# Another road into the 2x2 product: two plain blocks first, conditioning beside it, a small inversion on GpSimd

## Chip, core and metric

One core of a Trainium2 chip runs the whole program in one launch. The metric is the device time in microseconds (us). The kernel before was run three times; one further execution was recorded by the hardware profiler, and all rows below come from it.

## What is computed

Two layers of a hybrid backbone over 1152 tokens (128 context and 1024 latent) of width 1024. Cut to what matters here:

```python
m = silu(cond) @ w_ada + b_ada          # per layer: 6 vectors of 1024, for two conditionings (ctx, lat)
h = modulate(rms_norm(x, g), m[0], m[1])
x = x + m[2] * mix(h)                   # layer 0: neighbourhood + differential attention
                                        # layer 1: retention + RWKV-7 scan in both directions
h = modulate(rms_norm(x, g), m[3], m[4])
g, u = split(h @ w_ffn_in)              # D_FF = 2816
x = x + m[5] * ((silu(g) * u) @ w_ffn_out)
# at the end one rms_norm; fp32 throughout
```

## The kernel before

TensorE works in fp32r: every fp32 operand is split into a high and a low part (a cast on ScalarE and a subtraction on VectorE or GpSimd), and each product is three matmuls. The program is written as generators and ordered by a list scheduler when it is built: the order on each engine is fixed in advance by planned times, and each engine's queue then runs in that order and waits where something is late. DMAs are issued from SyncE's queue (SP) in one order too.

The parts that the diff touches, in order of time:

- **Layer 0's conditioning**, column groups 4 to 11 of 512 columns (`ada_steps`, lines 187 to 203), beside the differential attention. A step loads a [128 x 512] tile of `w_ada` (`aw`, line 133), splits it (ScalarE line 140, GpSimd line 141) and issues two matmuls with four stationary columns (line 148). After 8 steps `ada_end` copies the [4 x 512] sum and turns it (line 160). `pull` gives 0.28 steps per slot.
- **FFN of each layer** (`ffn`, lines 1656 to 1821). `w_ffn_in` is worked through in 22 column blocks f. Block 0 is plain: `mm3` over 8 row tiles for 3 token groups of 384 columns and for gate and up, 144 matmuls. From block 1 on, a Winograd-like 2x2 scheme makes 7 products instead of 8: each product is 24 matmuls of 288 columns, so 168 in a block. It needs combinations of the activations, which `forms` (lines 1823 to 1867) makes once on VectorE, GpSimd and ScalarE in 24 units: T1 and T2 (8 units), T3 (8) and a last sum (8) that overwrites a part of `hH`, `hL`. Each product is taken out of PSUM banks A, B, E, D by ScalarE and VectorE. Results go to DRAM (`hdr`).
- **FFN out** (`ffn_out`, lines 1869 to 1928) reads `hdr` and `w_ffn_out` through the ring of 6 `raw` tiles, 1584 matmuls of 384 columns. In layer 0, layer 1's conditioning runs beside it (`ada_vec`, lines 205 to 232): per step one `aw` tile out of the same ring, two VectorE operations that add it, times a scalar, to `aacc`; every 8 steps 8 fp32 matmuls with a column of ones (line 230).
- **Layer 1's scan** (`rec_scan`): 18 rounds m of `prep`, `amat`, `inv16`, `values`, `levels`, `chain`, interleaved by a written order. `inv16` (lines 1220 to 1256) inverts 16x16 triangular blocks: the blocks go to DRAM and come back block by partition (`bts`, `BT`), a copy (line 1232), 15 rounds of a multiplication (line 1241) and an addition (line 1242) on VectorE with at most 64 elements in a partition, a copy and an addition (lines 1244 and 1245), and again through DRAM (`mbs`, `ML`). `BT` and `MB` have one buffer each.

```python
for j in range(15):
    nc.vector.tensor_tensor(tt, row, col, op=ALU.mult)
    nc.vector.tensor_tensor(M3[:, j + 1 :, :ncl], M3[:, j + 1 :, :ncl], tt, op=ALU.add)
```

Of the kernel before, what the change touches and what calls it, by code (L numbers as in the profile page):

```python
# [44 lines left out]
class Net:  # L45
# [41 lines left out]
    def setup(self, top):  # L87
# [32 lines left out]
        self.cond = self.t(c, [P, KT, 4], F32R, tag="cond")  # L120
        cv = self.v2[:, 0:16].rearrange("p (c k) -> p k c", c=2)
        self.split(self.cond[:, :, 0::2], self.cond[:, :, 1::2], cv)
        self.comb = self.t(c, [4, 2], tag="comb")
        nc.scalar.dma_start(self.comb, I["k_comb"])
# [11 lines left out]
    def ada_split(self, w, n, pool, eng=None):  # L136
        nc = self.nc
        wh = self.t(pool, [P, n, 512], F32R, tag="awh")
        wl = self.t(pool, [P, n, 512], F32R, tag="awl")
        nc.scalar.copy(wh, w)  # L140
        (eng or nc.gpsimd).tensor_tensor(wl, w, wh, op=ALU.subtract)  # L141
        return wh, wl

    def ada_mm(self, pt, k, n, ws):
        wh, wl = ws
        for i in range(n):
            for ww in (wh, wl):
                self.nc.tensor.matmul(
                    pt[0:4, :], lhsT=self.cond[:, k + i, :], rhs=ww[:, i, :], start=k + i == 0 and ww is wh, stop=k + i == KT - 1 and ww is wl
                )  # L150

    def ada_end(self, l, cg, pt, pool, ps, r=4):

        nc = self.nc
        s4 = self.t(pool, [r, 512], tag="as4", bufs=1)
        nc.scalar.copy(s4, pt[0:r, :])
        p2 = self.t(ps, [P, 512], tag="mm")
        comb = self.comb if r == 4 else self.ident[0:2, 0:2]
        for f in range(4):
            nc.tensor.matmul(p2[:, 2 * f : 2 * f + 2], lhsT=s4[:, f * P : (f + 1) * P], rhs=comb, start=True, stop=True)  # L160
        self.ada_mod(l, cg, p2)
# [14 lines left out]
    def ada(self, l, cg, pool, ps, n):  # L176

        pt = self.t(ps, [P, 512], tag="mm")
        cond = self.v2[:, 0:16].rearrange("p (c k) -> p k c", c=2)
        for k in range(0, KT, n):  # L180
            w = self.ada_load(l, cg, k, n, pool)
            for i in range(k, k + n):
                self.nc.tensor.matmul(pt[0:2, :], lhsT=cond[:, i, :], rhs=w[:, i - k, :], start=i == 0, stop=i == KT - 1)
        self.ada_end(l, cg, pt, pool, ps, 2)

    def ada_steps(self, l, cgs, pool, ps, eng=None):

        seq = [(cg, k) for cg in cgs for k in range(KT)]
        raw, spl, pt = {}, {}, None
        for i in range(-3, len(seq)):  # L190
            if i + 3 < len(seq):
                raw[i + 3] = self.ada_load(l, *seq[i + 3], 1, pool)
            if 0 <= i + 2 < len(seq):
                spl[i + 2] = self.ada_split(raw.pop(i + 2), 1, pool, eng)
            if i >= 0:
                cg, k = seq[i]
                if k == 0:
                    pt = self.t(ps, [P, 512], tag="ada")
                self.ada_mm(pt, k, 1, spl.pop(i))
                if k == KT - 1:  # L200
                    self.ada_end(l, cg, pt, pool, ps)
                yield

    def ada_vec(self, l, cgs, pool):


        nc = self.nc
        seq = [(cg, k) for cg in cgs for k in range(KT)]
        raw, acc = {}, None
        for i in range(-1, len(seq)):  # L210
            if i + 1 < len(seq):
                raw[i + 1] = self.ada_load(l, *seq[i + 1], 1, pool)
            if i < 0:
                continue
            cg, k = seq[i]
            w = raw.pop(i)[:, 0, :]
            if k == 0:
                acc = self.t(pool, [P, 2, 512], tag="aacc", bufs=1)
            for c in range(2):
                s = self.v2[:, c * 8 + k : c * 8 + k + 1]  # L220
                if k == 0:
                    nc.vector.tensor_scalar_mul(acc[:, c, :], w, s)
                else:
                    nc.vector.scalar_tensor_tensor(acc[:, c, :], w, s, acc[:, c, :], op0=ALU.mult, op1=ALU.add)  # L224
            if k == KT - 1:
                p2 = self.t(self.nps, [P, 512], tag="mm")
                for f in range(4):
                    for c in range(2):
                        o = p2[:, 2 * f + c : 2 * f + c + 1]
                        nc.tensor.matmul(o, lhsT=acc[:, c, f * P : (f + 1) * P], rhs=self.ones, start=True, stop=True)  # L230
                self.ada_mod(l, cg, p2)
            yield

# [827 lines left out]
    def rec_scan(self, hp):  # L1061
        nc, I, O = self.nc, self.I, self.O
        hp.release()
        with ExitStack() as es:
# [155 lines left out]
            def inv16(m):  # L1220
# [16 lines left out]
                for j in range(15):  # L1237
# [3 lines left out]
                    nc.vector.tensor_tensor(tt, row, col, op=ALU.mult)  # L1241
                    nc.vector.tensor_tensor(M3[:, j + 1 :, :ncl], M3[:, j + 1 :, :ncl], tt, op=ALU.add)  # L1242
# [413 lines left out]
    def ffn(self, l, x, hH, hL, p, tp, cs, ps, side, last):  # L1656
# [24 lines left out]
        cw = {}  # L1681
        for u in range(2):
            for a in range(2):
                w, c = raw(0, a, u), slice((u * 2 + a) * 512, (u * 2 + a + 1) * 512)
                cw[u, a] = T["T3h"][:, c], T["T3l"][:, c]
                self.split(*cw[u, a], w)
        forms = self.forms(hH, hL, ops, _Cycle(cs), p)
        pg = []
        for tg in range(TG):
            sl = slice(tg * GW, (tg + 1) * GW)  # L1690
            for u in range(2):
                pt = self.t(ps, [P, 512], tag="mm")
                for k in range(KT):
                    wh, wl = (w[:, (k % 4) * P : (k % 4 + 1) * P] for w in cw[u, k // 4])
                    self.mm3(pt[:, :GW], wh, wl, hH[k][:, sl], hL[k][:, sl], k == 0, k == KT - 1)
                pg.append(pt)
                self.tail_step()
        for tg in range(TG):
            for _ in itertools.islice(forms, (4, 2, 2)[tg]):
                pass  # L1700
            s = self.t(p, [P, GW], tag="c")
            nc.scalar.activation(s, pg[2 * tg][:, :GW], AF.Silu)
            nc.vector.tensor_tensor(s, s, pg[2 * tg + 1][:, :GW], op=ALU.mult)
            nc.sync.dma_start(self.hdr[0][:, tg * GW : (tg + 1) * GW], s)
# [52 lines left out]
        load(1, (0, 0), (1, 0), (0, 1), (1, 1))  # L1757
        prep(1, 0)
        prep(1, 1)
        seq = [(f, i) for f in range(1, NF) for i in range(7)]  # L1760
        out2 = self.ffn_out(l, x, hH, hL, p, T, ps, wo, side, last)
        C, store = {}, []
# [55 lines left out]
        for d, s in store:  # L1818
            nc.sync.dma_start(d, s)
        for _ in out2:  # L1820
# [143 lines left out]
    def run(self):  # L1964
        tc, nc, I = self.tc, self.nc, self.I
        self.tail = iter(())
        with ExitStack() as top:
# [8 lines left out]
            def ahead():  # L1976
                wp = wes.enter_context(self.pool("wA", side="right"))
                self.wpool = _Bufs(wp, {"wraw": 3, "wh": 9, "wl": 9, "ist": 2, "aw": 2, "awh": 3, "awl": 3})
# [21 lines left out]
    def attn(self, hp, hH, hL, wes):  # L2000
# [16 lines left out]
        GS, AS, OS = 0.28, 0.28, 0.34  # L2017
# [5 lines left out]
        with ExitStack() as es:  # L2023
            ps = _Mux(_Bufs(es.enter_context(self.pool("psA", space=PSUM)), {"S": 1, "ada": 1}), bps, ("mm", "T", "o"), {"S": "bba"})
# [7 lines left out]
            ada = self.ada_steps(0, range(4, 12), wpool, ps)  # L2032
# [258 lines left out]
```

## Time and profile before

| | |
|---|---|
| runs, median (lowest to highest) | 3959.39 us (3959.38 to 3960.79) |
| the profiled execution, its own time | 3954.28 us |
| its span | 3952.3 us |
| mean granted TensorE clock | 0.964 |
| busy: TensorE, VectorE, ScalarE, GpSimd | 94%, 60%, 37%, 28% |

Busy time is the union of an engine's instructions. A matmul's row spans its whole way through the array, so matmuls overlap and a busy TensorE is not one at its peak; counts of matmuls in a stretch tell more. The granted clock is a share of 2.4 GHz (0.5 is the lower level of 1.2 GHz).

### The profile page before, as it was taken

Reading aid. Unit: us, or ns where it says so; the run is one execution under the profiler, and the core shown is the slowest. Engines: PE = TensorE matmul, PEld = TensorE weight load, DVE = VectorE, ACT = ScalarE, POOL = GpSimd, SP = SyncE. Lnnn points to the kernel's source line nnn. Section 1 sums busy time; section 2 is a strip of 40 time slices with the busy share of each in tenths; the row PEclk is TensorE's granted clock in tenths of the full one; section 3 lists DMA queues with packets and bytes.
Section 4 is the critical chain, followed back from the end, with each engine's and each line's share of the span. In section 5 each row is a group of like instructions: output and inputs, shape, how many; then the busy total and the mean of one; then the engine's idle time right before and its main releaser. Section 6 shows DMA issues by size and latency. Waiting matters only on the chain.

```text
span 3952.3 us, 67315 instructions
## 1 busy us (share of the span) xinstructions
PE 3709.5 (94%) x24997; PEld 3465.6 (88%) x24997; DVE 2362.6 (60%) x5461; ACT 1457.2 (37%) x3454; POOL 1128.2 (29%) x1064
## 2 busy tenths in 40 slices
PE   8999998999899999999999997888888989999998
PEld 5899997999799999999989886777767879999998
DVE  5566665666744448885253657888875774444434
ACT  4555545555333341115222323232222533334221
POOL 3322202103532233332020322233332453223430
PEclk9999998999899999999999997999998989999999
DMA  6532316431122225543333435222223112222431
GB/s 204 151 101 83 106 56 157 128 94 49 51 77 73 76 87 171 166 149 114 102 118 98 167 103 167 70 63 74 68 52 96 51 54 74 73 78 89 127 91 60
DMA packets 425695, 392.16 MB, mean 99 GB/s; under 512 B 68212, under 2 KB 370672, under 8 KB 423832
## 3 DMA queue, kind: packets, MB, share of 16 engines
q1 hardware_dynamic: 406928, 376.29, 31.2%
q10 hardware_dynamic: 13160, 7.27, 0.7%
q0 software_dynamic: 5280, 4.31, 0.5%
q8 instruction: 197, 3.23, 0.3%
q14 instruction: 130, 1.06, 0.1%
HBM read 289.32 MB, written 98.33 MB: 98 GB/s over the span
## 4 chain that ended last, share of the span: by engine, by line
PE 54%; DVE 12%; DMA 5%; issue 2%; POOL 1%; ACT 1%; SPq 0%; DVEq 0%; ACTq 0%; POOLq 0%
PE mm L82 6%; PE mm L84 6%; PE mm L83 6%; PE A L1745 3%; PE A L1747 3%; PE A L1746 3%; PE E L1747 2%; PE E L1745 2%; PE E L1746 2%; DVE c L1827 1%; PE mm L858 1%; DVE MB L1242 1%; PE mm L860 1%; PE mm L859 1%; PE A L1191 1%
## 5 line engine op out<-in xcount | busy, mean ns | idle before, releaser
L770 DVE SCALAR_TENSOR_TENSOR x<-mm,mod,x 128x128 f32<-128x128 f32 (+1 forms) x576 | 278.9, 511 | 213.5 <-PE mm L84 212.3
L1677 POOL TENSOR_TENSOR wl<-raw,wh 128x512 fp32r<-128x512 f32 x126 | 172.1, 1366 | 588.3 <-ACT wh L1676 584.0
L1676 ACT CAST wh<-raw 128x512 fp32r<-128x512 f32 x294 | 182.2, 620 | 346.6 <-PE A L1746 123.1
L391 PE MATMUL mm<-wh,hH 128*128 128x384 f32 x576 | 199.1, 346 | 3.0 <-ACT ist L409 3.0
L392 PE MATMUL mm<-wl,hH 128*128 128x384 f32 x576 | 195.1, 339 | 0.0
L393 PE MATMUL mm<-wh,hL 128*128 128x384 f32 x576 | 193.7, 338 | 0.0
L75 DVE TENSOR_TENSOR wl<-wraw,wh 128x256 fp32r<-128x256 f32 (+1 forms) x184 | 95.7, 540 | 114.2 <-ACT wh L74 86.4
L82 PE MATMUL mm<-hH,wh 128*128 128x384 f32 x432 | 152.5, 354 | 2.8 <-ACT wh L74 2.8
L1191 PE MATMUL A<-AR,BK 64*128 64x256 f32 x576 | 125.6, 438 | 30.5 <-DVE tf L1241 11.1
L84 PE MATMUL mm<-hH,wl 128*128 128x384 f32 x432 | 148.7, 346 | 2.9 <-DVE rst L908 2.4
L1719 DVE TENSOR_TENSOR raw<-raw,raw 128x512 f32<-128x512 f32 x42 | 30.9, 737 | 200.8 <-POOL raw L1718 200.8
L1677 DVE TENSOR_TENSOR wl<-raw,wh 128x512 fp32r<-128x512 f32 x168 | 120.1, 715 | 48.6 <-ACT wh L1676 46.5
L224 DVE SCALAR_TENSOR_TENSOR aacc<-aw,v,aacc 128x512 f32<-128x512 f32 x168 | 148.7, 920 | 0.0
L82 PE MATMUL mm<-mh,owh 128*128 128x384 f32 x384 | 141.1, 382 | 7.6 <-ACT mh L74 5.3
L83 PE MATMUL mm<-hL,wh 128*128 128x384 f32 x432 | 148.1, 344 | 0.0
L84 PE MATMUL mm<-mh,owl 128*128 128x384 f32 x384 | 133.5, 348 | 2.0 <-DVE owl L75 2.0
L83 PE MATMUL mm<-ml,owh 128*128 128x384 f32 x384 | 135.4, 353 | 0.0
L141 POOL TENSOR_TENSOR awl<-aw,awh 128x512 fp32r<-128x512 f32 x64 | 88.2, 1387 | 158.5 <-ACT awh L140 107.0
L1191 PEld LDWEIGHTS A<-AR,BK 64*128 64x128 f32 x576 | 82.2, 208 | 55.0 <-issue 15.5
L1790 DVE TENSOR_TENSOR c<-c,B 128x288 f32<-128x288 f32 x84 | 38.1, 454 | 153.5 <-PE B L1747 83.4
L565 ACT ACTIVATE P<-S,mx 128x384 f32<-128x384 f32 (+1 forms) x200 | 111.9, 569 | 45.6 <-DVE mx L563 45.6
L858 PE MATMUL mm<-wh,hH 128*128 128x256 f32 x432 | 124.0, 290 | 0.0
(553 smaller groups left out, 13019.2 us busy)
## 6 DMA issues: line engine op xcount, KB each, us to landing
raw<-in_w_ffn_in_dram SPq DMA_DIRECT2D x176, 256.0 KB
aw<-in_w_ada_dram SPq DMA_DIRECT2D x160, 256.0 KB
raw<-hdr SPq DMA_DIRECT2D x132, 192.0 KB
hdr<-c SPq DMA_DIRECT2D x168, 144.0 KB
raw<-in_w_ffn_out_dram SPq DMA_DIRECT2D x88, 256.0 KB
F<-stg SPq DMA_DIRECT2D x34, 640.0 KB
stg<-st SPq DMA_DIRECT2D x12, 1536.0 KB
qkv<-ist SPq DMA_DIRECT2D x72, 192.0 KB
```

What stands on the lines that cost most here:

```text
L82: mm(out, lhsT=wh, rhs=xh, start=first, stop=False)
L83: mm(out, lhsT=wh, rhs=xl, start=False, stop=False)
L84: mm(out, lhsT=wl, rhs=xh, start=False, stop=last)
L391: mm(pt[:, :ncol], lhsT=hH[k][:, c], rhs=WH[k], start=k == 0, stop=False)
L392: mm(pt[:, :ncol], lhsT=hH[k][:, c], rhs=WL[k], start=False, stop=False)
L393: mm(pt[:, :ncol], lhsT=hL[k][:, c], rhs=WH[k], start=False, stop=k == KT - 1)
L770: self.nc.vector.scalar_tensor_tensor(x[f][:, c], pt[:, a:b], self.mod[l][jg][:, f, cd : cd + 1], x[f][:, c], op0=ALU.mult, op1=ALU.add)
L1191: mm(pts[h][:, j * 256 : j * 256 + 256], lhsT=BK[hs, j, :], rhs=AR[hs], start=True, stop=True)
L1677: eng.tensor_tensor(wl, w, wh, op=ALU.subtract)
L1745: mm(o, lhsT=wh[:, ks], rhs=xh, start=new and k == 0, stop=False, skip_group_check=True)
L1746: mm(o, lhsT=wh[:, ks], rhs=xl, start=False, stop=False, skip_group_check=True)
L1747: mm(o, lhsT=wl[:, ks], rhs=xh, start=False, stop=k == 3, skip_group_check=True)
```

## The change

Four edits. (1) Layer 0's conditioning runs as `ada_vec` on VectorE, at 0.3 steps per slot, with two `aw` tiles; its PSUM bank goes to the attention's scores `S`. (2) The FFN's block 1 is plain too, and the forms are spread over both plain blocks and the first 2x2 products; the 2x2 scheme starts at block 2; the loads for the next block are regrouped. (3) Layer 1's conditioning runs beside the 2x2 products from block 3 on, at 0.82 steps per product, no longer beside FFN out; it has one `aw` tile of its own, layer 0's `raw` ring has 5 tiles, and the sum of a column group uses PSUM bank D. `ada_vec` loads the next tile after the operations of the last, and reads a finished sum one step later. (4) The two operations of the inversion's rounds are issued on GpSimd.

```diff
@@ ada_vec
-        for i in range(-1, len(seq)):
-            if i + 1 < len(seq):
-                raw[i + 1] = self.ada_load(l, *seq[i + 1], 1, pool)
...
+        w, acc, p2 = self.ada_load(l, cgs[0], 0, 1, pool), None, None
+        for n, cg in enumerate(cgs):
+            for k in range(KT):
+                if k == 0:
+                    if p2 is not None:
+                        self.ada_mod(l, cgs[n - 1], p2)
+                    acc = self.t(pool, [P, 2, 512], tag="aacc", bufs=1)
+                for c in range(2):
+                    s = self.v2[:, c * 8 + k : c * 8 + k + 1]
+                    if k == 0:
+                        nc.vector.tensor_scalar_mul(acc[:, c, :], w[:, 0, :], s)
+                    else:
+                        nc.vector.scalar_tensor_tensor(acc[:, c, :], w[:, 0, :], s, acc[:, c, :], op0=ALU.mult, op1=ALU.add)
+                if k < KT - 1 or n < len(cgs) - 1:
+                    w = self.ada_load(l, *((cg, k + 1) if k < KT - 1 else (cgs[n + 1], 0)), 1, pool)
+                yield
+            p2 = self.t(self.nps, [P, 512], tag="mm")
...
@@ inv16
-                    nc.vector.tensor_tensor(tt, row, col, op=ALU.mult)
-                    nc.vector.tensor_tensor(M3[:, j + 1 :, :ncl], M3[:, j + 1 :, :ncl], tt, op=ALU.add)
+                    nc.gpsimd.tensor_tensor(tt, row, col, op=ALU.mult)
+                    nc.gpsimd.tensor_tensor(M3[:, j + 1 :, :ncl], M3[:, j + 1 :, :ncl], tt, op=ALU.add)
@@ ffn (third, evac: the plain block as before, as functions)
+        w0 = [split(raw(1, a, 0), nc.vector) for a in range(2)]
         for tg in range(TG):
-            for _ in itertools.islice(forms, (4, 2, 2)[tg]):
-                pass
...
+            evac(0, tg, *pg[2 * tg : 2 * tg + 2])
+            form((4, 2, 0)[tg])
+        pg = [third(w0, tg) for tg in range(TG)]
+        w1 = [split(raw(1, a, 1), nc.vector) for a in range(2)]
+        form(4)
+        for tg in range(TG):
+            pu = third(w1, tg)
+            form(2)
+            evac(1, tg, pg[tg], pu)
...
-        seq = [(f, i) for f in range(1, NF) for i in range(7)]
+        seq = [(f, i) for f in range(2, NF) for i in range(7)]
...
+        self.nps = _Alias(ps.pool, {"mm": "D"})
...
-            for _ in itertools.islice(forms, 4):
-                pass
+            form(3)
...
-            elif i == 2:
-                load(f + 1, (1, 0))
             elif i == 5:
-                load(f + 1, (0, 1), (1, 1))
+                load(f + 1, (1, 0), (0, 1), (1, 1))
+            if n >= 7:
+                due += 0.82
+                while due >= 1:
+                    due -= 1
+                    next(side, None)
@@ attn
-        GS, AS, OS = 0.28, 0.28, 0.34
+        GS, AS, OS = 0.28, 0.3, 0.34
-            ps = _Mux(_Bufs(es.enter_context(self.pool("psA", space=PSUM)), {"S": 1, "ada": 1}), bps, ("mm", "T", "o"), {"S": "bba"})
+            ps = _Mux(_Bufs(es.enter_context(self.pool("psA", space=PSUM)), {"S": 2}), bps, ("mm", "T", "o"), {"S": "ba"})
-            ada = self.ada_steps(0, range(4, 12), wpool, ps)
+            ada = self.ada_vec(0, range(4, 12), wpool)
@@ ffn_block
-            p = _Bufs(es.enter_context(self.pool(f"ff{l}", "right" if l else "left")), {"raw": 6, "wh": 3, "wl": 3, "c": 4})
+            p = _Bufs(es.enter_context(self.pool(f"ff{l}", "right" if l else "left")), {"raw": 6 if l else 5, "wh": 3, "wl": 3, "c": 4})
-            side = iter(()) if l else self.ada_vec(1, range(12), _Alias(p, {"aw": "raw"}))
+            side = iter(()) if l else self.ada_vec(1, range(12), p)
```

## Rows read from the trace of the kernel before

**Rows 1.** The page: span, engines' busy us; a group's count, busy us, mean ns.

```profile
span 3952.3 us, 67315 instructions
...
PE 3709.5 (94%) x24997; PEld 3465.6 (88%) x24997; DVE 2362.6 (60%) x5461; ACT 1457.2 (37%) x3454; POOL 1128.2 (29%) x1064
...
L224 DVE SCALAR_TENSOR_TENSOR aacc<-aw,v,aacc 128x512 f32<-128x512 f32 x168 | 148.7, 920 | 0.0
```

**Rows 2.** Windows: stretch, length, busy us (instructions), granted clock, DMA share, GB/s.

```profile
110.00:590.00 480.00, 465.59 (x2960) 440.46 (x2961) 305.16 (x754) 252.43 (x766) 105.56 (x98) 0.99 0.33 99
990.00:1040.00 50.00, 32.27 (x163) 28.59 (x162) 47.49 (x67) 16.72 (x39) 34.51 (x34) 0.73 0.08 24
1050.00:1480.00 430.00, 430.00 (x3235) 429.60 (x3235) 189.74 (x347) 161.67 (x335) 131.18 (x100) 1.00 0.25 78
1490.00:1785.00 295.00, 282.46 (x1601) 280.07 (x1602) 242.21 (x398) 57.20 (x105) 99.73 (x82) 0.95 0.51 160
2425.00:2955.00 530.00, 461.70 (x3641) 379.72 (x3642) 436.85 (x1296) 150.16 (x351) 160.75 (x172) 0.95 0.23 61
3160.00:3210.00 50.00, 32.11 (x154) 28.77 (x152) 46.64 (x67) 17.08 (x40) 33.93 (x34) 0.73 0.08 24
3660.00:3910.00 250.00, 250.00 (x1444) 250.00 (x1443) 100.62 (x198) 51.26 (x96) 83.63 (x79) 1.00 0.29 87
```

**Rows 3.** The chain that ended last, 2839 to 2872 us: start, us, what.

```profile
2840.39 0.28 DVE BT L1244
...
2841.92 3.35 DMA mbs<-BT
...
2846.30 1.78 DMA BT<-bts
...
2848.20 1.00 DVE BT L1232
...
2870.57 0.28 DVE BT L1244
```

**Rows 4.** Lines 1232 and 1241: count, ns min/median/max, first and last start.

```profile
L1232 DVE COPY BT<-BT x18: 283/620/1257, 2421.9 to 2936.5; 32x256 f32<-32x256 f32 x18
...
L1241 DVE TENSOR_TENSOR tf<-BT,MB x270: 155/201/1265, 2423.2 to 2951.8; 64x15 f32<-64x15 f32 x18, 64x39 f32<-64x39 f32 x18, 64x55 f32<-64x55 f32 x18, 64x63 f32<-64x63 f32 x18
```

**Rows 5.** GpSimd's groups by form, 2425 to 2955 us: busy us, mean ns, idle before.

```profile
L1168 POOL TENSOR_TENSOR BK<-F,EN 128x512 f32<-128x512 f32 x30 | 38.8, 1295 | 128.4 <-ACT BH L1171 50.3 <-issue 40.7 <-ACT X L1278 26.0
...
L1166 POOL TENSOR_TENSOR AR<-F,EL 128x256 f32<-128x256 f32 x30 | 22.3, 742 | 34.7 <-PE c L1337 34.7
```

**Rows 6.** Timeline, 2604 to 2608 us, VectorE and GpSimd: start, us.

```profile
2606.50 0.73 POOL L1166 TENSOR_TENSOR AR<-F,EL 128x256 f32<-128x256 f32 x1 [0.89 <-PE c L1337]
...
2606.57 0.72 DVE L1241 TENSOR_TENSOR tf<-BT,MB 64x48 f32<-64x48 f32 x1
```

**Rows 7.** TensorE's waits, 940 to 1060 us: total, times, longest.

```profile
PE A L1745 <- ACT T3h L1856: 8.5, 1, 8.5
```

**Rows 8.** Groups of instructions, 100 to 600 us: count, busy us, mean ns.

```profile
L148 PE MATMUL ada<-awl,cond 128*4 128x512 f32 x64 | 25.5, 398 | 1.3 <-POOL awl L141 1.1
...
L160 PE MATMUL mm<-comb,as 4*128 4x2 f32 x64 | 8.4, 249 | 1.9 <-ACT ist L409 1.9
```

**Rows 9.** Timeline of TensorE, 1702 to 1708 us.

```profile
1704.29 1.84 PE L230 MATMUL mm<-ones,aacc 128*128 128x1 f32 x16
1705.99 0.42 PE L82 MATMUL mm<-T3h,hH 128*128 128x384 f32 x1
```

**Rows 10.** Line 224 on VectorE: count, ns min/median/max, first and last start.

```profile
L224 DVE SCALAR_TENSOR_TENSOR aacc<-aw,v,aacc x168: 732/743/1831, 1485.6 to 1766.3; 128x512 f32<-128x512 f32 x168
```

**Rows 11.** Timelines of SyncE's queue and ScalarE, 330 to 360 us.

```profile
335.82 0.34 SPq L133 DMA_DIRECT2D aw<-in_w_ada_dram  x1
...
339.07 0.62 ACT L140 CAST awh<-aw 128x512 fp32r<-128x512 f32 x1 [2.29 <-DMA aw<-in_w_ada_dram]
```

**Rows 12.** SyncE's own waits, 1480 to 1790 us: total, times, longest.

```profile
SPq L133 <- DMA raw<-hdr: 16.0, 14, 2.8
```

More of the change, by code (lines that the diff above doesn't have):

```diff
@@ L134, in ada_load, with ada_end @@
         return w
-    def ada_split(self, w, n, pool, eng=None):
+    def ada_end(self, l, cg, pt, pool, ps):
         nc = self.nc
[L138 to L156, printed above, removed]
+        s2 = self.t(pool, [2, 512], tag="as2", bufs=1)
+        nc.scalar.copy(s2, pt[0:2, :])
         p2 = self.t(ps, [P, 512], tag="mm")
-        comb = self.comb if r == 4 else self.ident[0:2, 0:2]
+        comb = self.ident[0:2, 0:2]
         for f in range(4):
-            nc.tensor.matmul(p2[:, 2 * f : 2 * f + 2], lhsT=s4[:, f * P : (f + 1) * P], rhs=comb, start=True, stop=True)
+            nc.tensor.matmul(p2[:, 2 * f : 2 * f + 2], lhsT=s2[:, f * P : (f + 1) * P], rhs=comb, start=True, stop=True)
         self.ada_mod(l, cg, p2)
@@ L183, in ada @@
                 self.nc.tensor.matmul(pt[0:2, :], lhsT=cond[:, i, :], rhs=w[:, i - k, :], start=i == 0, stop=i == KT - 1)
[L184 to L202, printed above, removed]
+        self.ada_end(l, cg, pt, pool, ps)
@@ new lines, in ada_vec @@
+        w, acc, p2 = self.ada_load(l, cgs[0], 0, 1, pool), None, None
+        for n, cg in enumerate(cgs):
+            for k in range(KT):
+                if k == 0:
+                    if p2 is not None:
[11 more added lines that the diff above has]
+            p2 = self.t(self.nps, [P, 512], tag="mm")
+            for f in range(4):
+                for c in range(2):
+                    o = p2[:, 2 * f + c : 2 * f + c + 1]
+                    nc.tensor.matmul(o, lhsT=acc[:, c, f * P : (f + 1) * P], rhs=self.ones, start=True, stop=True)
@@ L232, in ada_vec @@
             yield
+        self.ada_mod(l, cgs[-1], p2)
     @staticmethod
@@ L1678, in split, with evac, third, form @@
             return wh, wl
-        cw = {}
+        def evac(f, tg, g, u):
+            s = self.t(p, [P, GW], tag="c")
+            nc.scalar.activation(s, g[:, :GW], AF.Silu)
+            nc.vector.tensor_tensor(s, s, u[:, :GW], op=ALU.mult)
+            nc.sync.dma_start(self.hdr[f][:, tg * GW : (tg + 1) * GW], s)
+        def third(w, tg):
+            pt = self.t(ps, [P, 512], tag="mm")
+            sl = slice(tg * GW, (tg + 1) * GW)
+            for k in range(KT):
+                wh, wl = (v[:, (k % 4) * P : (k % 4 + 1) * P] for v in w[k // 4])
+                self.mm3(pt[:, :GW], wh, wl, hH[k][:, sl], hL[k][:, sl], k == 0, k == KT - 1)
+            return pt
+        def form(n):
+            for _ in itertools.islice(forms, n):
+                pass
+        cw = [[], []]
         for u in range(2):
@@ L1689, in ffn @@
         for tg in range(TG):
-            sl = slice(tg * GW, (tg + 1) * GW)
             for u in range(2):
[L1692 to L1696, printed above, removed]
+                pg.append(third(cw[u], tg))
                 self.tail_step()
+        w0 = [split(raw(1, a, 0), nc.vector) for a in range(2)]
         for tg in range(TG):
-            for _ in itertools.islice(forms, (4, 2, 2)[tg]):
-                pass
[L1701 to L1704, printed above, removed]
+            evac(0, tg, *pg[2 * tg : 2 * tg + 2])
[7 more added lines that the diff above has]
+            evac(1, tg, pg[tg], pu)
         cs = _Cycle(cs)
@@ L1756, in ffn @@
         wo = I["w_ffn_out"][l]
-        load(1, (0, 0), (1, 0), (0, 1), (1, 1))
-        prep(1, 0)
-        prep(1, 1)
-        seq = [(f, i) for f in range(1, NF) for i in range(7)]
+        load(2, (0, 0), (1, 0), (0, 1), (1, 1))
+        prep(2, 0)
+        prep(2, 1)
+        seq = [(f, i) for f in range(2, NF) for i in range(7)]
         out2 = self.ffn_out(l, x, hH, hL, p, T, ps, wo, side, last)
-        C, store = {}, []
+        C, store, due = {}, [], 0.0
+        self.nps = _Alias(ps.pool, {"mm": "D"})
         H2 = HT // 2
```

35 lines of the change are left out of this document (5 added, 30 removed).

## The prediction

> **What bounds the kernel now.** I read the page first: TensorE is busy 94% of the span [rows 1], but that is a mean over stages, so I cut the span into stretches. In the windows [rows 2] the reader should compare the count of matmuls, not the busy time. In the FFN's 2x2 products (1050 to 1480) TensorE runs without a gap at clock 1.00: 430 us / 3235 = 0.133 us per matmul of 288 columns; layer 1's FFN out (3660 to 3910) does the same, 250 / 1444 = 0.173 us per matmul of 384. These two are the full rates. Against them three places lose time.
>
> First, the beginning of both FFNs: 163 matmuls in 50 us (990 to 1040) where the full rate needs 163 x 0.133 = 21.7 us, so 28.3 us are lost, and in layer 1 (3160 to 3210) 154, so 29.5 us. VectorE is busy 47.5 of these 50 us; the largest single wait of TensorE is 8.5 us for T3 [rows 7], and its clock in the stretch is 0.73, so it fell to the lower level after such gaps. Second, layer 0's FFN out (1490 to 1785) has VectorE at 82% and TensorE's clock at 0.95; of its 1601 matmuls 192 are the narrow ones of line 230. Third, layer 1's scan: TensorE 87%, VectorE 82%.
>
> For the scan I read the chain [rows 3]: from the copy out of one inversion (2840.39) through two DMAs to the copy into the next (2848.20) are 7.8 us, and the inversion itself takes until 2870.57, 22.4 us, because its 30 short operations stand between other work of VectorE. Together 30.2 us. The copies of line 1232 start from 2421.9 to 2936.5 [rows 4], 17 periods of 30.3 us. So this ring, with one buffer for `BT`, sets the scan's pace.
>
> **Edit 4, the inversion on GpSimd.** GpSimd takes 1295 ns for 512 columns and 742 ns for 256 [rows 5], so 2.16 ns per column and 189 ns at no columns. The 15 rounds have (15 - j)(j + 1) elements, 680 in all, 45 on average: 0.29 us per operation, 8.6 us for 30. The ring becomes 7.8 + 1.0 + 8.6 = 17.4 us. That no row shows so short a GpSimd operation leaves bounds: twice the price gives 26 us, still under 30.3. TensorE is late next: 461.7 us busy in 530 are 26.4 us per period. VectorE falls from 437 by 17 x 30 x 0.29 us, the busy time at about that price each, = 148, to some 55%; GpSimd rises from 9.2 to 17.8 us per period, and what stands behind the inversion in its queue (the BK, AR, E and MM products of `prep` and `levels`) can be up to 8.6 us later; TensorE waits for those. So at most 17 x (30.3 - 26.4) = 66 us, at least nothing; I take 45, nearer to the upper end since the ring falls so far below TensorE's 26.4.
>
> One row limits this: at 2606.57 VectorE's 48-element product took 0.72 us instead of the median 0.20 [rows 4], ending with a GpSimd operation begun at 2606.50 [rows 6]. The two engines exclude each other here. The Trainium skill says so too (SBUF — State Buffer, Who interferes with whom): a VectorE operation with two SBUF inputs and a GpSimd operation that reads SBUF block each other for a whole instruction, whoever came first. By that rule the short operations, now on GpSimd, would wait behind VectorE's long ones; it is the second rival below.
>
> **Edit 2, two plain blocks.** A plain block costs 144 x 0.173 = 24.9 us, a 2x2 block 168 x 0.133 = 22.3, so TensorE gets 2.6 us more in each FFN. In return 24.9 us of matmuls that need no forms run while VectorE makes them. The forms are bound by VectorE (47.5 of 50 us) and end no earlier; the new block puts four splits and three multiplications before them, 7 operations of 512 columns or fewer, at the 0.743 us of such a two-input operation [rows 10] 5.2 us. When the forms end, one whole block more is done: 22.3 - 5.2 = 17 us per FFN. Bounds: 28.3 - 2.6 = 26 if no gap is left, 10 if the forms are later. Two FFNs: -34.
>
> **Edit 3, layer 1's conditioning moved.** In FFN out, 1601 - 192 = 1409 matmuls at 0.173 are 244 us; a column group's 16 narrow ones take 1.70 us [rows 9], twelve groups 20.4. The stretch has 295, so 31 us are stalls and lower clock, and layer 1's FFN out, without conditioning, has none. I take -29 (the ring of 5 tiles then serves 66 loads of `hdr` and 44 of weights, and no longer 96 of `aw`). The narrow matmuls move along, +20.4 and -20.4.
>
> The price stands in the 2x2 products. VectorE: 190 us in 430 now, and 192 x 0.743 = 143 us more [rows 10], in 133 products x 24 x 0.133 = 424 us: 44% + 34% = 78%. That would fit. But there is one `aw` tile: the next load is issued after both operations on the last. From issue to use a load takes 339.07 - 335.82 = 3.25 us [rows 11], the two operations 1.49, so a step lasts 4.74 us. Eight are 37.9 us, and 0.82 steps per product of 3.19 us leave 9 / 0.82 x 3.19 = 35.0 for a column group: 12 x 2.9 = 35 us late. The late operation holds VectorE's queue, and behind it are the evacuations of A, B, E and D, for which TensorE waits. Lower bound 0: if the planned order lets the conditioning slip, it ends in FFN out, where VectorE has 60% to spare. With the 148.7 / 168 = 0.885 us per operation that it took in FFN out [rows 1], 5.02 us a step, 62 us late. I take +25. The loads regrouped at i = 5 have three products, 9.6 us, before their use, and go in here.
>
> The Trainium skill asks for two buffers so that transfers overlap with computing (Trainium Kernel Development and Optimization, Best Practices). By that rule a step would last as long as the longer of its two parts, and the 35 us would be none; here they add up, and the rule speaks against this piece of the change.
>
> **Edit 1, layer 0's conditioning on VectorE.** Removed from TensorE: 2 x 64 matmuls of 512 columns [rows 8], at 0.173 x 512 / 384 = 0.231 us 29.5, and line 160, 8.4. Added: 8 groups x 1.70 = 13.6. Net -24, in a stage where TensorE is busy 466 of 480 us. ScalarE and GpSimd lose their splits, VectorE gets 128 x 0.743 = 95 us: 305 + 95 in some 456, 88%. In its queue the maxima of the scores stand behind these operations, and ScalarE's exponentials and so TensorE wait for them. Bounds -24 to +10 (a third of the 95 us exposed); a fourth bank for `S` helps. I take -14.
>
> The rest (setup, constants) is a few short operations: 0.
>
> **Sum.** -45 - 34 - 29 + 25 - 14 = -97; from the profiled execution's own 3954.3 that gives 3857. The median of the runs lies 5 us above that execution, so I say 3862 us. A measurement of this kernel tells about 0.2%, 8 us, from no change.
>
> **Rivals.**
> *The one tile throttles the FFN (other side).* Without the +25 the gains are 122 us. They are gone when a step lasts (12 x 35.0 + 122) / 96 = 5.65 us. With 0.885 per operation it is 5.02, and behind other DMAs SyncE's queue held an `aw` load 16.0 / 14 = 1.1 us longer [rows 12]: 6.1 us. Then the FFN is 96 x 6.1 - 420 = 166 us late, and the time 3959 - 122 + 166 = 4003 us. For it: VectorE's order is fixed in advance, so a late load stops all that is behind it. Against it: the order is planned with some time for each load, so the conditioning may slip instead. Chance 0.07, and 0.10 for a throttle between (3925 to 3951).
>
> *The scan stays as it is.* If each of the 30 short operations waits half the time behind a VectorE operation of 0.743 us, the ring is 17.4 + 11 = 28 us, and the delays of BK and E take the rest: 3862 + 45 = 3907 us. Chance 0.16. For it: rows 6. Against it: VectorE is free half of the time then.
>
> *All goes well.* No throttle (-25), the scan at TensorE's pace (-21), the attention at -24 (-10): 3806 us. Chance 0.19. For it: from 1050 to 1480 no evacuation ever held TensorE. Against it: there VectorE had 56% to spare, and now 22%.
>
> *Likeliest* (the sum, its own range 3825 to 3895): 0.48. Range over the cases, 8 in 10: 3785 to 3940. Left out are the slow throttle, a third of the middle one and the best end of the best case, 0.16. Faster 0.90, same 0.03 (part of the middle throttle), slower 0.07.
>
> **What would show it.** Right: lines 1241 and 1242 on GpSimd at about 0.3 us, copies of line 1232 some 27 us apart; at the FFN's head no wait for T3 and some 17 us less from the first plain matmul to the second 2x2 block; layer 0's FFN out without gaps at clock 1.00, like layer 1's; 2x2 products at 0.133 us per matmul plus the narrow ones. Wrong: VectorE waiting on the `aw` DMA in the 2x2 products and TensorE on VectorE's evacuations, GpSimd's short operations stretched towards 0.7 us, or TensorE waiting for maxima in the attention.

## The result, and the profile after

The changed kernel takes 3919.9 us (median of four runs, 3912.0 to 3924.3) against 3959.5 us: ratio 0.9897, 95% interval 0.9878 to 0.9916. It is faster by 1.0%, in the direction forecast, but by 40 us and not by 97. The profiled execution is the one of 3924.3 us, with a span of 3922.5 us.

To find the missing 57 us I cut both traces at the same matmuls (first and last starts and ends of each kind, in the views by tile) and set the forecast of each stretch beside it:

| stretch, us | before | after | change | forecast |
|---|---|---|---|---|
| start to layer 0's first FFN matmul | 956.3 | 957.4 | +1.1 | -14 |
| layer 0's FFN: plain blocks and 2x2 products | 529.5 | 612.6 | **+83.1** | +28 (-17 + 20.4 + 25) |
| layer 0's FFN out | 329.4 | 278.3 | -51.1 | -49 (-29 - 20.4) |
| retention, projections | 567.4 | 569.6 | +2.2 | 0 |
| scan | 614.6 | 563.0 | -51.6 | -45 |
| to layer 1's FFN | 130.7 | 129.9 | -0.8 | 0 |
| layer 1's FFN: plain blocks and 2x2 products | 529.9 | 517.9 | -12.0 | -17 |
| layer 1's FFN out, end | 294.5 | 293.9 | -0.6 | 0 |

One row holds most of the error. The page of the changed kernel names the suspect at once; of line 181 (the conditioning on VectorE, both layers) it says that VectorE stood idle before it for 134.9 us, nearly all of it for the load of `aw`, and the largest wait of TensorE in a group of 2x2 products is for VectorE:

```profile
span 3922.5 us, 67157 instructions
PE 3687.0 (94%) x24885; PEld 3458.7 (88%) x24885; DVE 2292.8 (58%) x5026; ACT 1397.8 (36%) x3361; POOL 1161.5 (30%) x1530
...
L181 DVE SCALAR_TENSOR_TENSOR aacc<-aw,v,aacc 128x512 f32<-128x512 f32 x280 | 230.1, 856 | 134.9 <-DMA aw<-in_w_ada_dram 134.5
...
L1721 PE MATMUL E<-hH,wh 128*128 128x288 f32 x320 | 102.1, 319 | 28.2 <-DVE c L1783 28.0
```

The windows of the changed kernel (stretch, length, busy time and instructions of each engine, granted clock, DMA share, GB/s) answer to [rows 2]. Compare the first and the last row: the same 2x2 products, with the conditioning beside them (layer 0, 2657 matmuls in 400 us, the narrow ones included, clock 0.97) and without (layer 1, 3008, clock 1.00). The second row is layer 0's FFN out, now without a gap, and the third the scan:

```profile
1060.00:1460.00 400.00, 367.92 (x2657) 361.67 (x2657) 260.64 (x422) 114.43 (x254) 105.13 (x77) 0.97 0.37 107
1580.00:1800.00 220.00, 220.00 (x1270) 220.00 (x1269) 84.33 (x166) 45.73 (x87) 76.56 (x73) 1.00 0.29 86
2470.00:2930.00 460.00, 431.41 (x3521) 359.54 (x3520) 312.27 (x717) 144.93 (x344) 284.99 (x662) 0.97 0.25 68
3200.00:3600.00 400.00, 400.00 (x3008) 400.00 (x3008) 175.76 (x322) 147.15 (x305) 119.89 (x91) 1.00 0.25 75
```

The waits from 1050 to 1570 us (total, times, longest) show the chain of two links: VectorE waits for the load, TensorE waits for VectorE.

```profile
PE E L1721 <- DVE c L1783: 28.0, 14, 5.7
PE A L1723 <- DVE wl L1636: 12.5, 9, 2.3
...
DVE aacc L181 <- DMA aw<-in_w_ada_dram: 122.6, 65, 5.1
```

The timelines of VectorE and SyncE's queue show one turn of the ring: load issued at 1280.32, operations from 1283.11 for 1.42 us, the next load issued at 1284.56, 0.03 us after they end, operations from 1287.45, the next load at 1288.89. VectorE sits idle for 1.85 and 2.92 us in between:

```profile
1283.11 1.42 DVE L181 SCALAR_TENSOR_TENSOR aacc<-aw,v,aacc 128x512 f32<-128x512 f32 x2 [1.85 <-DMA aw<-in_w_ada_dram]
1287.45 1.41 DVE L181 SCALAR_TENSOR_TENSOR aacc<-aw,v,aacc 128x512 f32<-128x512 f32 x2 [2.92 <-DMA aw<-in_w_ada_dram]
...
1280.32 0.33 SPq L128 DMA_DIRECT2D aw<-in_w_ada_dram  x1
...
1284.56 0.33 SPq L128 DMA_DIRECT2D aw<-in_w_ada_dram  x1
...
1288.89 0.33 SPq L128 DMA_DIRECT2D aw<-in_w_ada_dram  x1
```

The chain that ended last (1100 to 1300 us; start, us, what) joins these turns to TensorE: load, operations, the next load issued as they end, three times over, then an evacuation on VectorE and the product of A that needed it.

```profile
1264.62 2.79 DMA aw<-in_w_ada_dram
...
1267.43 2.98 DVE aacc L181 x2
...
1270.43 3.37 DMA aw<-in_w_ada_dram
...
1275.88 2.91 DMA aw<-in_w_ada_dram
...
1280.30 0.37 DVE c L1769
...
1281.47 0.40 PE A L1721
```

The view of line 128 gives the mean of such turns (count, ns, first and last start): 87 loads from 1093.2 to 1547.5, so 454.3 / 86 = 5.28 us.

```profile
L128 SPq DMA_DIRECT2D aw<-in_w_ada_dram x87: 327/328/341, 1093.2 to 1547.5; - x87
```

Of the 96 loads the other nine were issued earlier (same view, 950 to 1000 us):

```profile
L128 SPq DMA_DIRECT2D aw<-in_w_ada_dram x9: 328/328/341, 955.3 to 998.3; - x9
```

So the planned order put VectorE's work for the first column group beside the plain blocks, ahead of the 2x2 products at which its steps are called. Eleven of the twelve groups ran beside the 2x2 products, not all twelve. The same holds for every run below that uses the changed `ada_vec`.

In the scan the first operation of the inversion, now on GpSimd, and the copy into each inversion answer to [rows 4]: 0.26 us each, and 18 copies from 2455.9 to 2925.6, 17 periods of 27.6 us.

```profile
L1200 POOL TENSOR_TENSOR tf<-BT,MB x270: 207/261/1187, 2457.9 to 2938.0; 64x15 f32<-64x15 f32 x18, 64x39 f32<-64x39 f32 x18, 64x55 f32<-64x55 f32 x18, 64x63 f32<-64x63 f32 x18
...
L1191 DVE COPY BT<-BT x18: 283/284/941, 2455.9 to 2925.6; 32x256 f32<-32x256 f32 x18
```

### The profile page after: what moved, and what is told of

The parts are those of the page before. It is cut to its first block, busy times and chain, and to the rows that moved or that the text cites. A ratio compares the mean times of both kernels' runs of the same rounds, so it can differ in the third digit from the quotient of the medians.

```text
span 3922.5 us, 67157 instructions
## 1 busy us (share of the span) xinstructions
PE 3687.0 (94%) x24885; PEld 3458.7 (88%) x24885; DVE 2292.8 (58%) x5026; ACT 1397.8 (36%) x3361; POOL 1161.5 (30%) x1530
## 4 chain that ended last, share of the span: by engine, by line
PE 51%; DVE 6%; DMA 5%; POOL 2%; issue 2%; ACT 1%; DVEq 0%; SPq 0%; POOLq 0%; ACTq 0%
PE mm L82 7%; PE mm L84 7%; PE mm L83 7%; DMA aw<-in_w_ada_dram 2%; PE A L1723 2%; PE A L1721 2%; PE A L1722 2%; PE mm L817 1%; PE E L1721 1%; PE mm L818 1%; PE E L1722 1%; PE E L1723 1%; PE mm L819 1%; PE A L1150 1%; DVE aacc L181 1%
## 5 line engine op out<-in xcount | busy, mean ns | idle before, releaser
L181 DVE SCALAR_TENSOR_TENSOR aacc<-aw,v,aacc 128x512 f32<-128x512 f32 x280 | 230.1, 856 | 134.9 <-DMA aw<-in_w_ada_dram 134.5
L82 PE MATMUL mm<-hH,wh 128*128 128x384 f32 x528 | 187.2, 355 | 10.9 <-ACT wh L1635 8.3
L84 PE MATMUL mm<-hH,wl 128*128 128x384 f32 x528 | 182.2, 347 | 3.0 <-DVE rst L867 2.4
L83 PE MATMUL mm<-hL,wh 128*128 128x384 f32 x528 | 182.5, 346 | 0.0
L397 POOL TENSOR_TENSOR rm<-rm,rm 128x128 f32<-128x128 f32 (+1 forms) x40 | 28.1, 702 | 460.7 <-DVE rm L387 328.9
L1636 DVE TENSOR_TENSOR wl<-raw,wh 128x512 fp32r<-128x512 f32 x168 | 129.8, 773 | 43.4 <-ACT wh L1635 42.2
L1721 PE MATMUL E<-hH,wh 128*128 128x288 f32 x320 | 102.1, 319 | 28.2 <-DVE c L1783 28.0
L350 PEld LDWEIGHTS mm<-wh,hH 128*128 128x128 f32 x576 | 110.0, 191 | 15.9 <-ACT ist L368 7.0
```

The lines of the kernel that those rows point to most:

```text
L82: mm(out, lhsT=wh, rhs=xh, start=first, stop=False)
L83: mm(out, lhsT=wh, rhs=xl, start=False, stop=False)
L84: mm(out, lhsT=wl, rhs=xh, start=False, stop=last)
L181: nc.vector.scalar_tensor_tensor(acc[:, c, :], w[:, 0, :], s, acc[:, c, :], op0=ALU.mult, op1=ALU.add)
L350: mm(pt[:, :ncol], lhsT=hH[k][:, c], rhs=WH[k], start=k == 0, stop=False)
L1636: eng.tensor_tensor(wl, w, wh, op=ALU.subtract)
```

## The experiments

All start from the changed kernel. The diffs are shortened: `...` stands for what is left out, and `op` and `load` for the calls. The theory, "round trip": with one tile a load and the operations on it take turns; the steps are called closer together than a turn lasts, VectorE's queue stands still for the load, and what is queued behind it (the evacuations, the splits) reaches TensorE late. The rivals: VectorE has too much work; the loads' traffic is in the way of the weights; the regrouped weight loads come late; and for the terms of the scan and the attention, that the gain has another cause. The table gives the time, its ratio to the kernel before, and two stretches of the profiled run, 2x2 from the first 2x2 product to the last:

| run | median us (lowest to highest) | ratio, 95% interval | 2x2, layer 0 | FFN out, layer 0 |
|---|---|---|---|---|
| the change | 3919.9 (3912.0 to 3924.3) | 0.9878 to 0.9916 | 546.9 | 278.3 |
| two half tiles | 3913.3 (3911.3 to 3927.2) | 0.9881 to 0.9930 | 540.8 | 279.2 |
| all beside FFN out, one tile | 4001.5 (3992.8 to 4002.8) | 1.0095 to 1.0130 | 458.9 | 446.1 |
| inversion on VectorE | 3967.9 (3955.8 to 3977.5) | 1.0022 to 1.0048 | 539.5 | 278.9 |
| pace 0.6 | 3909.0 (3907.2 to 3911.7) | 0.9869 to 0.9899 | 517.3 | 301.2 |
| one load only | 3855.1 (3844.1 to 3855.7) | 0.9700 to 0.9774 | 484.6 | 278.3 |
| steps placed | 3908.4 (3905.3 to 3915.8) | 0.9852 to 0.9913 | 522.1 | 295.0 |
| half tiles, placed | 3919.4 (3913.5 to 3924.0) | 0.9876 to 0.9938 | 524.6 | 298.0 |
| layer 0's conditioning back | 3917.9 (3907.8 to 3936.2) | 0.9874 to 0.9938 | 543.1 | 278.3 |
| edit 3 undone | 3884.7 (3871.2 to 3900.5) | 0.9781 to 0.9862 | 455.4 | 332.2 |
| spread | 3868.5 (3857.6 to 3882.1) | 0.9745 to 0.9817 | 484.1 | 294.9 |
| two steps ahead | 3866.0 (3852.7 to 3871.9) | 0.9735 to 0.9801 | 479.7 | 284.4 |
| loads unread | 3907.1 (3900.0 to 3917.7) | 0.9848 to 0.9920 | 522.7 | 278.3 |

**Two half tiles** of 256 columns in the memory of one (`W` is 256, `parts` 2):

```diff
-    for c in range(2): ... op(acc[:, c, :], w[:, 0, :], s)
-    w = self.ada_load(...)
+    for h in range(parts):
+        for c in range(2): ... op(acc[:, c, h * W : (h + 1) * W], ws[h], s)
+        ws[h] = load(..., h)
```

> Layer 1's conditioning stays beside the 2x2 products of layer 0's FFN, but its one tile of 512 columns is cut into two of 256 (the same memory), each loaded anew as soon as its own two operations are done. Theory 'round trip': the step of load and operations (5.28 us in the changed kernel, 86 of them) sets the pace of the stretch, because what VectorE has queued behind a late load waits too. Then the two halves overlap, VectorE's 123 us of waiting on the load fall under 40, the 547 us from the first 2x2 product to FFN out fall to some 480, and the time is 3850 to 3865 us. Rival 'VectorE's work': the 143 us of operations themselves are too much beside the evacuations; the half tiles make them twice as many and a little longer, and the time is 3915 to 3935.

A miss for the theory. The time lies within the spread of the changed kernel's runs and 2 us below the rival's range, so this run speaks for VectorE's work rather than against it. From 1050 to 1560 us VectorE still waits 68.6 us for loads and TensorE 29.1 us for the addition on E. Worked out afterwards: a half turns round in a load of some 2.9 us and two operations of 0.478, 3.9 us, and at 0.82 most steps are one product, 3.2 us, apart. Halving the tile doesn't put a load further ahead. That explanation is argued, not tested here.

**All beside FFN out**, still with one tile:

```diff
-    if n >= 7:
+    if n >= 7 and l > 1:
         due += 0.82
```

> The conditioning of layer 1 is taken off the 2x2 products and runs beside layer 0's FFN out, as in the kernel before, with the one tile. Theory 'round trip': the stretch of 2x2 products falls from 547 to 447 us (3360 x 0.133), FFN out rises from 278 to some 315 to 330 us, as VectorE has 60% to spare there and TensorE waits for little of it; the time is 3860 to 3875 us. Rival 'the regrouped loads': the three weight loads now issued together three products before their use hold the products up, so the stretch stays above 480 us without any conditioning, and the time is above 3890.

The first half came as expected: without conditioning the products take 458.9 us, so the regrouped loads are no cause, and the conditioning (eleven groups of operations and loads, all twelve groups' narrow matmuls) costs 547 - 459 = 88 us there. The second half was far off: FFN out takes 446 us. Moved with its one tile, the throttle moves along; there TensorE waits for the narrow matmuls' input directly (windows and TensorE's waits of this run):

```profile
1490.00:1920.00 430.00, 334.03 (x1729) 325.88 (x1727) 239.74 (x423) 71.74 (x143) 104.13 (x95) 0.83 0.37 111
```

```profile
PE mm L189 <- DVE aacc L181: 76.7, 11, 19.5
PE mm L82 <- DVE x L729: 14.0, 7, 3.0
```

VectorE is busy 56% of that stretch and waits 120.7 us of it for the loads, so it isn't its work.

**The inversion back on VectorE**, lines 1200 and 1201:

```diff
-    nc.gpsimd.tensor_tensor(tt, row, col, op=ALU.mult)
+    nc.vector.tensor_tensor(tt, row, col, op=ALU.mult)
```

> The inversion of the scan goes back to VectorE, nothing else is undone. If the ring of the inversion made the gain of the scan (563 us after, 615 before), the scan takes some 615 again and the time is 3965 to 3978 us. Rival: the scan got shorter by something else (a different order or lengths of loads), then the time stays within 15 us of 3920.

As expected: the scan takes 608.4 us and the time is 48 us above the changed kernel's. The copies into the inversion, by the view of line 1191, are (2959.0 - 2443.4) / 17 = 30.3 us apart, as in [rows 4]:

```profile
L1191 DVE COPY BT<-BT x18: 283/990/1256, 2443.4 to 2959.0; 32x256 f32<-32x256 f32 x18
```

Without this edit the other three leave the kernel slower than before, by 0.2 to 0.5%.

**Pace 0.6** instead of 0.82:

```diff
-                due += 0.82
+                due += 0.6
```

> The steps of the conditioning are called at 0.6 per 2x2 product instead of 0.82, one per 5.3 us of products instead of 3.9; about a third of them is left for FFN out. Theory 'round trip': a step of 4.3 to 5.3 us now fits, VectorE waits for few loads and the stretch falls from 547 to some 465 to 480 us, FFN out rises by 10 to 15 us; the time is 3855 to 3875 us. Rival 'VectorE's work': what holds TensorE is in proportion to the operations in the stretch, so two thirds of some 80 us stay, and the time is 3895 to 3910.

A miss for the theory, and the rival's forecast came: the time lies in its range, and of the 88 us 517 - 459 = 58 stay, two thirds. 30 us are gained in the products and 23 given back in FFN out. It need not be the work, though: at 0.6 a third of the steps still stand at neighbouring products, and VectorE waits 89 us for loads (1050 to 1560 us). The run leaves both open.

**One load only**, to leave the work and take away the wait:

```diff
-                if k < KT - 1 or n < len(cgs) - 1:
+                if l == 0 and (k < KT - 1 or n < len(cgs) - 1):
                     w = self.ada_load(
```

> In layer 1's conditioning only the first weight tile is loaded and all 96 steps read it (that part of the result is left out); VectorE's 192 operations, the narrow matmuls and their places stay. Theory 'round trip' (VectorE's queue stands still for the load): without any load to wait for, the stretch of 2x2 products falls from 547 to 470 to 485 us (3360 x 0.133 + 20.4 and little more), time 3840 to 3860 us. Rival 'VectorE's work' (the operations themselves, and the GpSimd operations that they exclude, make the evacuations late): the stretch stays above 515 us and the time above 3890. The half tiles, which took away only 6 us, and the pace of 0.6, which took away 30 us but gave 23 back in FFN out, leave both open.

Time and stretch lie in the theory's ranges and far from the rival's. The window shows a TensorE without a gap beside the operations, with VectorE busier (73%) than in the changed kernel (65%). So the work by itself was not too much. The loads' traffic is gone here too, so this run can't tell it from the wait.

```profile
1060.00:1460.00 400.00, 399.94 (x3043) 399.48 (x3041) 291.80 (x489) 137.31 (x293) 122.14 (x87) 1.00 0.24 72
```

**Steps placed**, and **half tiles placed** the same way:

```diff
-            if n >= 7:
-                due += 0.82
-                while due >= 1: ...
+            if n >= 7 and i not in (4, 5):
+                next(side, None)
```

> One tile as in the changed kernel, but the steps are called at fixed products of a block: at products 0, 1, 2, 3 and 6, none at 4 and 5, where TensorE waits for the two additions on E (14 waits, 28 us). That is 5 steps per block of 22.3 us, or 21.5 us by the shortest step of 4.3; 18 of 108 are left for FFN out. Theory 'round trip at the narrow place': the waits for E's addition go, the stretch falls from 547 to 470 to 490 us, FFN out rises by 10 to 15, time 3865 to 3880 us. Rival 'VectorE's work': it falls only with the share of steps, to some 525 us, and the time is 3905 to 3915 as with the pace of 0.6.

> The two half tiles and the fixed places (products 0, 1, 2, 3, 6) together. Theory 'round trip': each half has a whole step for its load, so VectorE waits under 25 us on loads, the stretch is 470 to 480 us, FFN out has 2 groups left and is little longer (278 to 290), time 3850 to 3868 us. Rival 'VectorE's work': the half operations are 2 x 0.478 us in place of 0.750, so it is no better than the one tile at the same places, 3905 or more.

Both misses for the theory; both times, and the 522 us of the first, came out about where the rival had put them. After the run with one load only that can't be VectorE's work alone. TensorE waits for the addition on E 15 and 14 times as before (24.8 and 24.7 us), and VectorE for loads 104.5 and 62.5 us, so the place of a step within the block isn't what matters: four of the five steps are still 3.2 us apart.

**Layer 0's conditioning back** on TensorE, with its splits, `cond` and the bank for it:

```diff
-            ada = self.ada_vec(0, range(4, 12), wpool)
+            ada = self.ada_steps(0, range(4, 12), wpool, ps)
```

> Layer 0's conditioning goes back to TensorE as in the kernel before (the split, the matmuls with cond, the fourth bank); the other three edits stay. The changed kernel reached the first FFN 1 us later than the kernel before, so if that is this edit's whole effect the time stays within 8 us of 3920 (its first scores 7 us earlier, its attention 14 us longer, the second attention 8 us shorter). Rival, my prediction's term of -14 us: the edit gains 14 us and something else lost them, then the time is 3930 to 3940 us.

The first case: 2 us below the changed kernel, within the spread of the runs. The edit is worth nothing that can be measured here.

**Edit 3 undone**, the conditioning of before beside FFN out:

```diff
-            side = ... self.ada_vec(1, range(12), p)
+            side = ... self.ada_vec0(1, range(12), _Alias(p, {"aw": "raw"}))
```

> Layer 1's conditioning goes back beside layer 0's FFN out exactly as in the kernel before (one load ahead, in the ring of 6 raw tiles); the other three edits stay. By the stages already measured, the 2x2 stretch should take the 459 us that it takes without conditioning (547 with it) and FFN out the 329 us of before (278 after), so the move cost 37 us and the time is 3878 to 3893 us. Rival 'the move gained elsewhere': the time stays above 3905.

As expected, 35 us below the changed kernel. The same work beside the same FFN out takes 332 us with the load issued one step ahead, out of a ring of six tiles shared with FFN out, and 446 us with one tile beside a ring of five.

**Spread**: one tile, all loads and operations, but never two neighbouring products:

```diff
-            if n >= 7:
-                due += 0.82
-                while due >= 1: ...
+            if n >= 7 and i in (1, 3, 6):
+                next(side, None)
...
-                due += 0.8
+                due += 0.45
```

> One tile, all loads and operations as in the changed kernel, but a step only at products 1, 3 and 6 of a block, never at two products in a row (at least 6.4 us apart, where the shortest step is 4.3); the other half runs in FFN out at 0.45 per call instead of 0.8. Theory 'round trip': no step waits for its load and VectorE's queue never stands, so the stretch is 468 to 480 us, FFN out 290 to 305, time 3855 to 3880. Rival 'the loads' traffic' (the 24 MB themselves make the weight tiles of the products late): the stretch stays in proportion, above 500 us, and the time above 3890.

The time is in the forecast range, 51 us below the changed kernel; the stretch, 484 us, is 4 above its range and far below the 500 of the rival. TensorE's only waits of note from 1060 to 1460 us are these, and VectorE's idle time before line 181 is still there, 56 us, but harmless, since nothing behind it is due yet:

```profile
PE A L1723 <- DVE wl L1636: 6.4, 5, 1.3
PE E L1721 <- DVE c L1780: 0.9, 1, 0.9
```

**Two steps ahead**: groups of 256 columns, whose smaller accumulators free room for four tiles of 256 columns (the steps come at 0.93 per product instead of 0.82):

```diff
+        for n in range(4): load(n)
+        for n, (g, k) in enumerate(seq):
+            ... two operations of 256 columns on ws.pop(n)
+            load(n + 4)
+            if k % 2: yield
```

> The whole conditioning beside the 2x2 products, in groups of 256 columns: accumulators of 2 KB instead of 4, and in the memory that this frees four tiles of 256 columns, so that a load is issued two steps before its use. Twice as many operations, 0.478 us each, 40 us more of VectorE in all. Theory 'round trip': VectorE waits under 20 us for loads (123 before), the stretch is 470 to 490 us, time 3845 to 3870. Rival 'VectorE's work': with 183 us of operations the evacuations come late all the same, stretch above 515, time above 3895.

As expected, and 54 us below the changed kernel. Window and VectorE's wait for the load, 1060 to 1460 us:

```profile
1060.00:1460.00 400.00, 398.77 (x3033) 398.29 (x3033) 327.11 (x688) 128.91 (x286) 121.00 (x85) 1.00 0.42 127
```

```profile
DVE aacc L218 <- DMA aw<-in_w_ada_dram: 10.4, 11, 2.2
```

The reader is to see three things in one row: VectorE has more work than ever (82%), the DMAs move more than in any other version (127 GB/s), and TensorE has hardly a gap (1.2 us in 400) and clock 1.00. That excludes both the work and the traffic.

**Loads unread**: the operations read another tile.

```diff
-    nc.vector.scalar_tensor_tensor(acc[:, c, :], w[:, 0, :], s, ...)
+    nc.vector.scalar_tensor_tensor(acc[:, c, :], x[0][:, :512], s, ...)
```

> All 96 loads of the conditioning are issued into the one tile as before, but the 192 operations read a tile that has been in memory all along (that part of the result is left out), so traffic and VectorE's work stay and only the wait is gone. Theory 'round trip': as with one load only, the stretch is 480 to 490 us and the time 3845 to 3862. Rival 'the loads' traffic': it is the 24 MB beside the weight loads that cost, the stretch stays above 515 us and the time above 3890.

Stretch and time both lie in the rival's ranges, but the run didn't test what I meant. VectorE no longer waits for the loads; each load still waits for the one before it into the single tile, and this wait sits in SyncE's queue, ahead of the weight loads (waits of SyncE and VectorE, 1060 to 1460 us):

```profile
SPq L128 <- DMA aw<-in_w_ada_dram: 126.7, 61, 3.4
```

```profile
DVE raw L1696 <- POOL raw L1695: 53.9, 13, 11.8
```

What VectorE waits for now are the weights, by way of GpSimd, which waits three times as long for their loads as in the changed kernel (GpSimd's waits, 1060 to 1460 us, this run and the changed kernel):

```profile
POOL raw L1695 <- DMA raw<-in_w_ffn_in_dram: 78.0, 11, 14.9
```

```profile
POOL raw L1694 <- DMA raw<-in_w_ffn_in_dram: 26.5, 5, 7.6
```

So a wait at the single tile costs here too, 523 - 459 - 20 = 43 us, through another in-order queue. By itself this run doesn't exclude the traffic; the run with two steps ahead does. It also names a rival that I had not thought of: SyncE's queue stands at the load in the changed kernel as well (99.6 us for the load before, 82.4 for VectorE's operations). No run separates the two queues there. The traces speak for VectorE's: the 26.5 us for the weights are no more than the 24.5 with two steps ahead and the 27.5 with one load only, and the chain shown above runs through VectorE's operations.

## Why the prediction was right in sign and wrong in size

**The step that failed** is the price of edit 3 in the 2x2 products: "I take +25", with bounds 0 to 62. It measured 547 - 459 - 20 = 68 us, above the upper bound. The mechanism was the one described (the single tile, load and operations adding up, VectorE's queue behind it, TensorE waiting for the evacuations). What was mis-sized is the turn of a column group: eight turns of 4.74 us, 37.9, set against nine calls, 35.0. The seven turns within a group take 4.9 us on average, close to my sum (an operation that met one of GpSimd took up to 1.79 us instead of 0.75). The turn from one group to the next takes 8.2 us on average: a ninth call, which only issues the narrow matmuls, stands between, and I had counted its place as time that the loads could use. So a group takes 7 x 4.9 + 8.2 = 42.5 us, or 8 x 5.28 = 42.2 by the mean turn, and eleven groups are 11 x (42.2 - 35.0) = 80 us late, of the 88 measured with the narrow matmuls in them. (The mean is taken from the stretch itself, so this sum says where the time lies; that the wait for the load is its cause rests on the runs.) The timelines show such a turn, a load issued at 1298.47, used at 1305.57, the next one issued at 1306.48:

```profile
1298.47 0.33 SPq L128 DMA_DIRECT2D aw<-in_w_ada_dram  x1
...
1306.48 0.34 SPq L128 DMA_DIRECT2D aw<-in_w_ada_dram  x1
...
1305.49 0.17 DVE L149 TENSOR_TENSOR mod<-mm,v 128x8 f32<-128x8 f32 x1 [0.43 <-PE mm L189]
1305.57 0.88 DVE L179 TENSOR_SCALAR aacc<-aw,v 128x512 f32<-128x512 f32 x2
```

Then I shaved the 35 us to 25 because "the conditioning may slip". It did not slip into FFN out: the last operations start at 1550.97 us, before the last products. The one thing that moved is the first group, and it moved forward, beside the plain blocks.

Here the rival that I gave 0.10 ("a throttle between") came true in its mechanism, though not in its time (3925 to 3951). The rule of two buffers that I quoted (the Trainium skill, Trainium Kernel Development and Optimization, Best Practices) is borne out in part: two half tiles gained 7 us, which is within the spread of the runs, a load two steps ahead 54.

**Edit 1**, -14, measured nothing: +1.1 us in the traces, and undoing it makes the kernel 2 us faster, which is nothing. The term was right for the first attention, whose scores span 480.5 us instead of 493.9. It was given back on both sides, which I didn't cost: the first scores start 6.7 us later, and the second attention, whose start loads at a DMA share of 0.99 (640 to 660 us), takes 6.5 us longer from its first mask matmul to the FFN. That share was 0.87 before, so it is not shown to be the reason. In the twelve traces with edit 1 the first FFN matmul starts between 949.9 and 960.6 us, in the two without it at 956.3 and 955.9.

**Edit 2**, -17 per FFN, measured -12.0 in layer 1, where nothing else of the change runs: inside its bounds of 10 to 26. The wait for T3 is gone; in its place TensorE waits 3.5 us for the split of the new block's weights. In layer 0 the head and products without conditioning (edit 3 undone) take 519.3 us, 10 less than before.

**Edit 3's gain**, -29 in FFN out and the narrow matmuls moved, was right: -51.1 against -49.4, at clock 1.00 and 0.173 us per matmul (220 / 1270).

**Edit 4**, -45, was right and a little low: -51.6 in the traces, 48 by the run without it. GpSimd's short operations took 0.26 and 0.28 us against my 0.29, and the period 27.6 against 27. The rival "the scan stays" fell. The waiting that it rested on is there (line 1200 took up to 1.19 us, beside a VectorE operation of 1.51) but is rare: of the 540 short operations this one alone took over 0.6 us. One reading in this part was wrong: VectorE's relief was put at 148 us by GpSimd's 0.29 us for each of 510 operations; VectorE itself had taken 0.20 [rows 4], 102 us, and it is busy 312 of 460 us in the scan, 68% and not 55%.

Together, from the profiled executions: 83 - 28 = 55 us too much in layer 0's FFN, 15 in the attentions and 5 in layer 1's FFN, against 8 us better in scan and FFN out, make the 67 us between 3857 and 3924.

The version that beats both kernels is the one with the load two steps ahead, 3866.0 us, 0.9768 of the kernel before; the spread steps, 3868.5, can't be told from it. Both come out close to the 3862 that was forecast, and that is chance: the forecast had a throttle in it and they have none.

## What to carry to other kernels

A side job on an in-order queue costs by what it makes the work behind it wait, more than by what it works: before putting one there, compare the turn of its buffer (load, operations, and every call between that doesn't load) with the shortest distance between two of its steps, not with the mean. If the turn is longer, either issue the load a step further ahead or set the steps further apart; smaller pieces of the same buffer, loaded no further ahead, gained nothing here beyond the spread of the runs. And where a working sum already says that a ring is late, don't discount it for slack that no row shows.

## What the runs showed of the hardware that was not expected

A wait seems to cost more than its length, through the clock. In the run with all conditioning beside FFN out, TensorE's named waits are 76.7 + 14.0 + 5.2 us, but the stretch is 168 us longer than in the changed kernel, and the narrow matmuls are only 20 of them; 52 us are left over. The granted clock in it was 0.83, that is the level of 1.2 GHz for a third of the time, against 1.00 in the changed kernel's FFN out. That the clock makes up the 52 is worked out, not tested.

The scan's clock also differs between two kernels whose scan is the same code: with almost the same busy time of TensorE, 100 us of it had clock 0.86 with two steps ahead and 1.00 with the spread steps (first and second fence), and the scans took 582 and 557 us. What sets it off wasn't tried, and whether it is also why the four runs of one kernel lie some 20 us apart isn't shown, since there is one trace of each.

```profile
2650.00:2750.00 100.00, 94.81 (x692) 78.74 (x692) 61.94 (x146) 28.81 (x70) 59.30 (x137) 0.86 0.27 75
```

```profile
2665.00:2765.00 100.00, 93.55 (x808) 76.94 (x808) 67.30 (x159) 35.24 (x85) 64.96 (x146) 1.00 0.25 67
```
